# The pieces for sums of squares start at the fifth k-step of the first unit in the stage of seven products

## The chip, the cores and the metric

The kernel runs on one core of one Trainium2 chip. The time is that of one execution on the device, in microseconds (us). Three runs of the kernel before took 1785.42, 1786.99 and 1788.74 us, a median of 1786.99 us. The core has a matrix engine (PE, with its weight loads PEld as a row of their own), a vector engine (DVE), a scalar engine (ACT), a general engine (POOL), and a queue processor (SP) from which this kernel issues its DMA transfers.

## What is computed

One layer of an encoder over two groups of rows, 1024 "sample" rows and 256 "prompt" rows of 2048 features, each with 256 memory rows. The change concerns the scale of a root-mean-square norm, which is one number for each row of `x` and of `mem`:

```python
def rms_norm(x, g):
    xf = x.astype(jnp.float32)
    y = xf * lax.rsqrt(jnp.mean(xf * xf, axis=-1, keepdims=True) + EPS)
    return (y * g.astype(jnp.float32)).astype(x.dtype)

def layer(x, mem, norm_g, w_in, ..., w_out):
    hn = rms_norm(x, norm_g)
    proj = hn @ w_in
    xbc, z_ssd, dt_raw, q, k, v, z_att, mq, z_mem = split_cols(proj, IN_SIZES)
    ...
    memn = rms_norm(mem, mem_norm_g)
    mk, mv = split_cols(memn @ w_mem_kv, (MEM_WIDTH, MEM_WIDTH))
    ...
    return x + jnp.concatenate([o_ssd, o_att, o_mem], axis=-1) @ w_out
```

## The kernel before

Rows are handled in tiles of 128: ten of `x` (tiles 0 to 4 are the first group, 5 to 9 the second) and four of `mem`. Products are made in a split form: a weight or an activation is stored as a high part and a low part (`wh` and `wl`, `sh` and `sl`, `xH` and `xL`, `tH` and `tL`), and each product is three matmuls (lines 1240, 1241, 1242 in the stage of interest). `wsplit` (lines 206 and 207) makes the high part on ACT and the low part on DVE.

The order of the program is: keys and values of the memory rows, the block `q`, then **the stage of seven products**, and after that the attention, the scan, the gates and the output product.

**The stage of seven products** makes 14 units (`UNITS`), numbered u0 to u13 here. Each unit makes two blocks of 128 output features for the first and the second group of rows by seven products in place of eight. A unit has eight k-steps, and a k-step has 21 matmuls (seven products of three). The steps k=6 and k=7 are made product by product, so that each product ends in turn and its result is carried out while the others still run. `block_pair` loads the four weight blocks of a k-step (256 KB, tile `wraw`, line 1201), POOL makes three sums of them (tile `ws`, four instructions on line 1208), and `wsplit` makes `wh` and `wl` from `wraw`, `sh` and `sl` from `ws`. The tiles `wh` and `wl` have four buffers, `sh`, `sl` and `ws` three, `wraw` four. At the end of a unit `ev_seven` carries out the seven results; it begins with `yu`, an ACT copy (line 1330), and the rest is on DVE (lines 1332 to 1342). What is still to be done to a unit's results is put in the list `left` and done in small steps beside the next unit: a gate (`th`, stored to `zT` or `yT`) after u0, u2, u4 and so on, a convolution (`c` on line 362, `u` on line 368, stored to `xbc_d` on line 370) after u1, u3, u5 and so on up to u11.

**The pieces for sums of squares.** `stage_stats` goes through four tiles of `mem` and the tiles 5 to 9 of `x`, in pieces of 128 by 512: 36 pieces, four for a tile. For each piece there is a load (line 1392, tile `sst`), and an ACT instruction that squares it and sums along the row (line 1383). After the fourth piece of a tile DVE adds the four sums into `rx` (line 1386), and POOL makes the reciprocal root (lines 123 and 124). The pieces are in groups of three: a group takes four calls of `next(squares)`; the first call loads a piece, the second and third square one and load the next, the fourth squares the last. All pieces have one buffer, the tag `xst`, which they share with `wraw0` (the first weight block of the stage) ahead of them and with `yu` at the end of each unit. So a load waits for the square before it, the next group's first load waits until the last reader of `yu` is done (line 1340), and the very first load waits until `wraw0` has been split. The results `rx` are first read after the stage (`mk_prep`, `x_rows` of the second group).

**What sets the order.** The instructions of each engine are in a list that a scheduler makes: it takes the program as written, gives some parts a higher priority (`tc.high_priority`, used for the splits and for carrying out results), and lets an instruction go ahead of others where its own model of the engines says that it can start. Each engine then goes through its list strictly in order. DMA transfers are issued from the SP list in the same way: an issue that has to wait keeps all those behind it waiting.

The loop that the change touches, lines 1538 to 1554:

```python
    squares = stage_stats()
    owe = 0.0
    for u, unit in enumerate(units):
        for k in block_pair(w_in_pairs, u, rows_in, ev_seven(*unit), lead=2):
            if k in (0, 2, 4, 5):
                next(squares, None)

            owe = owe + (1.4 if k < 7 else 0.0) if left else 0.0
            while owe >= 1:
                owe -= 1
                if left:
                    some_left()
```

## Time and profile before

| what | us |
|---|---|
| median of three runs (lowest, highest) | 1786.99 (1785.42, 1788.74) |
| the profiled execution's own time | 1787.65 |
| its span, first to last instruction | 1785.9 |
| PE busy in the span | 1774.8 |
| DVE, ACT, POOL busy in the span | 1245.0, 921.6, 546.5 |

The seven products run from about 148.8 to 495.2 us of the span. The granted clock is 1.00 in this execution. Views of the trace are read as follows: a line of the timeline gives start, duration, engine, line and operation, the tiles written and read, how many such instructions in a row, and in brackets the idle time of the engine before it and what ended that; two numbers in a stretch's row are the engine's busy time and, in brackets, how many instructions it had. The ends of matmuls are modelled, and one starts before the one before it has ended: in the stage they start 0.146 us apart where nothing is waited for, though each is shown as some 0.31 us long.

### The profile page before, as it was taken

The numbers are of one execution on the slowest core, as the hardware profiler recorded it, in microseconds if no ns is written. First come the engines' busy times: TensorE is split into PE (matmuls) and PEld (weight loads), VectorE is DVE, ScalarE is ACT, GpSimd is POOL, SyncE is SP. The second block draws the span as 40 slices with busy tenths as digits, with TensorE's granted clock in tenths as the row PEclk, the third lists the DMA queues.
The fourth block names the chain that finished last, engine by engine and source line by source line (L and its number), as shares of the span: only waits on it lengthen the run. The fifth ranks groups of instructions, "written<-read, shape, count | busy, mean of one in ns | idle before, by whom it ended". The sixth has DMA issues, their size and how long they took to land.

```text
span 1785.9 us, 31408 instructions
## 1 busy us (share of the span) xinstructions
PE 1774.8 (99%) x10838; PEld 1606.1 (90%) x10838; DVE 1245.0 (70%) x2358; ACT 921.6 (52%) x2049; POOL 546.5 (31%) x900
## 2 busy tenths in 40 slices
PE   9999999999999999999999999999999999999999
PEld 7888999999998989999889977877988888899999
DVE  5596788888868877878665666557777644766665
ACT  5554455554434766756464565544447533533333
POOL 0105898988810100001001000000100000057775
PEclk9999999999999999999999999999999999999999
DMA  8554454445446644453635645557777754644442
GB/s 294 198 181 122 138 154 148 141 141 164 123 145 209 194 136 140 133 162 111 191 115 174 193 148 161 165 162 247 229 231 237 245 189 142 224 147 142 148 142 78
DMA packets 208207, 301.12 MB, mean 169 GB/s; under 512 B 19568, under 2 KB 86192, under 8 KB 208048
## 3 DMA queue, kind: packets, MB, share of 16 engines
q1 hardware_dynamic: 207904, 299.06, 54.0%
q8 instruction: 85, 1.39, 0.3%
q14 instruction: 74, 0.61, 0.1%
q10 hardware_dynamic: 144, 0.06, 0.0%
HBM read 236.36 MB, written 62.69 MB: 167 GB/s over the span
## 4 chain that ended last, share of the span: by engine, by line
PE 83%; DVE 5%; issue 5%; DMA 3%; POOL 2%; ACT 1%; SPq 0%; POOLq 0%; ACTq 0%; DVEq 0%
PE acc L258 9%; PE acc L260 9%; PE acc L259 9%; PE acc L1242 7%; PE acc L1240 7%; PE acc L1241 7%; PE acc L293 5%; PE acc L295 5%; PE acc L294 5%; PE accm L1241 3%; PE accm L1240 3%; PE accm L1242 3%; PE po L673 1%; PE ppt L663 1%; DVE wl L207 1%
## 5 line engine op out<-in xcount | busy, mean ns | idle before, releaser
L207 DVE TENSOR_TENSOR wl<-wraw,wh 128x512 fp32r<-128x512 f32 (+1 forms) x480 | 345.2, 721 | 244.0 <-ACT wh L206 234.9
L206 ACT ACTIVATE wh<-wraw 128x512 fp32r<-128x512 f32 (+1 forms) x480 | 292.2, 613 | 312.1 <-PE acc L260 148.4
L258 PE MATMUL acc<-wh,xH 128*128 128x512 f32 (+1 forms) x1088 | 418.7, 385 | 0.4 <-DVE v_all L337 0.4
L260 PE MATMUL acc<-wh,xL 128*128 128x512 f32 (+1 forms) x1088 | 410.0, 377 | 0.0
L259 PE MATMUL acc<-wl,xH 128*128 128x512 f32 (+1 forms) x1088 | 409.6, 376 | 0.0
L258 PEld LDWEIGHTS acc<-wh,xH 128*128 128x128 f32 x1088 | 204.5, 188 | 37.9 <-issue 3.3
L260 PEld LDWEIGHTS acc<-wh,xL 128*128 128x128 f32 x1088 | 204.2, 188 | 36.9 <-issue 0.2
L259 PEld LDWEIGHTS acc<-wl,xH 128*128 128x128 f32 x1088 | 204.7, 188 | 36.0 <-issue 1.6
L293 PE MATMUL acc<-xH,wh 128*128 128x320 f32 x640 | 202.7, 317 | 0.0
L294 PE MATMUL acc<-xL,wh 128*128 128x320 f32 x640 | 198.9, 311 | 0.0
L206 ACT ACTIVATE sh<-ws 128x384 fp32r<-128x384 f32 x176 | 91.3, 523 | 208.1 <-POOL ws L1208 108.9
L295 PE MATMUL acc<-xH,wl 128*128 128x320 f32 x640 | 198.0, 309 | 0.0
L207 DVE TENSOR_TENSOR sl<-ws,sh 128x384 fp32r<-128x384 f32 x176 | 124.4, 710 | 96.3 <-ACT sh L206 92.4
L1208 POOL TENSOR_TENSOR ws<-wraw 128x128 f32<-128x128 f32 x176 | 111.8, 635 | 209.0 <-DMA wraw<-in_w_in_pairs_dram 89.4
L635 POOL COPY lg<-nsink 128x2 f32<-128x2 f32 x40 | 13.8, 346 | 379.3 <-PE ppt L663 245.8
L293 PEld LDWEIGHTS acc<-xH,wh 128*128 128x128 f32 x640 | 120.2, 188 | 2.6 <-issue 2.2
L294 PEld LDWEIGHTS acc<-xL,wh 128*128 128x128 f32 x640 | 120.3, 188 | 1.7 <-issue 1.4
L1208 POOL TENSOR_TENSOR ws<-wraw,ws 128x128 f32<-128x128 f32 x176 | 117.5, 668 | 13.8
L295 PEld LDWEIGHTS acc<-xH,wl 128*128 128x128 f32 x640 | 120.2, 188 | 0.6 <-issue 0.5
L1208 POOL TENSOR_TENSOR ws<-ws,wraw 128x128 f32<-128x128 f32 x176 | 117.0, 665 | 0.0
L1208 POOL TENSOR_TENSOR wraw<-wraw 128x128 f32<-128x128 f32 x176 | 111.8, 635 | 13.7
L362 DVE SCALAR_TENSOR_TENSOR c<-u,vec,c 128x638 f32<-128x638 f32 (+1 forms) x96 | 90.0, 939 | 9.4 <-ACT c L357 9.0
(437 smaller groups left out, 3941.2 us busy)
## 6 DMA issues: line engine op xcount, KB each, us to landing
wraw<-in_w_in_laid_dram SPq DMA_DIRECT2D x176, 256.0 KB, 2.9
wraw<-in_w_in_pairs_dram SPq DMA_DIRECT2D x112, 256.0 KB, 2.7
wraw<-in_w_out_laid_dram SPq DMA_DIRECT2D x64, 256.0 KB, 3.3
wraw<-in_w_out_pairs_dram SPq DMA_DIRECT2D x64, 256.0 KB, 2.8
rf<-ac SPq DMA_DIRECT2D x40, 256.0 KB, 4.2
rb<-ac SPq DMA_DIRECT2D x40, 256.0 KB, 4.9
wraw<-in_w_mem_laid_dram SPq DMA_DIRECT2D x32, 256.0 KB, 4.7
xst<-in_x_sample_dram SPq DMA_DIRECT2D x20, 256.0 KB, 5.1
```

What stands on the lines that cost most here:

```text
L206: a = A.activation(h, raw, AF.Copy)
L207: b = V.tensor_sub(l, raw, h.bitcast(F32))
L258: T.matmul(ps[t][:, :n], sh, h[:, :n], start=(k_ == 0), stop=False)
L259: T.matmul(ps[t][:, :n], sh, l[:, :n], start=False, stop=False)
L260: T.matmul(ps[t][:, :n], sl, h[:, :n], start=False, stop=(k_ == KT - 1))
L293: T.matmul(o, sh, cur["H", q][:, m, c], start=(k == 0), stop=False)
L294: T.matmul(o, sh, cur["L", q][:, m, c], start=False, stop=False)
L295: T.matmul(o, sl, cur["H", q][:, m, c], start=False, stop=(k == KT - 1))
L1208: G.tensor_tensor(out=o, in0=x, in1=y, op=op)
L1240: T.matmul(ps[p], h, xh, start=(k_ == 0), stop=False)
L1241: T.matmul(ps[p], h, xl, start=False, stop=False)
L1242: T.matmul(ps[p], l, xh, start=False, stop=(k_ == 7))
```

## The change

In the first unit the calls of `next(squares)` at k=0 and k=2 are left out; those at k=4 and k=5 stay. In all other units the four calls stay as they were.

```diff
     for u, unit in enumerate(units):
         for k in block_pair(w_in_pairs, u, rows_in, ev_seven(*unit), lead=2):
-            if k in (0, 2, 4, 5):
+            if k in (4, 5) or u and k in (0, 2):
                 next(squares, None)
```

There are as many calls as the 36 pieces need, since there were 56 and are 54, and 48 do the work. By the written order each group of three now begins at k=4 of a unit and ends at k=2 of the next. What comes out in the engines' lists is shown at three places, in rows that give the line, the operation, the tiles written and read, and the shape. PE's list is the same in both.

The first place is ACT's list at the passage from the block `q` into u0. `qs` carries out the results of block `q`, `wh` and `sh` are splits for the seven products, `L1383` is a square, `tH` a part of the input rows. The piece of the difference:

```order
 L206 ACTIVATE wh<-wraw_1334 128x512
 L326 ACTIVATE qs<-acc 128x512 x2
-L1383 ACTIVATE sst,xs_1634<-sst 128x512
+L1383 ACTIVATE sst,xs_1752<-sst 128x512
 L326 ACTIVATE qs<-acc 128x512 x2
 L206 ACTIVATE wh<-wraw_1393 128x512
 L206 ACTIVATE wh<-wraw 128x512
 L326 ACTIVATE qs<-acc 128x512
-L1383 ACTIVATE sst,xs_1634<-sst 128x512
+L1383 ACTIVATE sst,xs_1752<-sst 128x512
 L206 ACTIVATE sh<-ws 128x384
 L1290 ACTIVATE tH<-ra 128x640
```

The two squares stand in the same two places as before, between the copies of `q` (only the number of the tile that takes the sums differs). The square that stood a few rows further on, third in u0, is no longer there; it comes next in u1.

The second place is SP's list just behind it: the stores of `q`, loads of weights (`wraw`), loads of pieces (`sst`), and the first store of a gate (`zT`).

```order
 L327 DMA q_126<-qs 128x512
 L327 DMA q_127<-qs 128x512
-L1201 DMA wraw<-in_w_in_pairs_dram 128x512
-L1392 DMA sst<-in_mem_sample_dram 128x512
-L1201 DMA wraw<-in_w_in_pairs_dram 128x512 x6
+L1201 DMA wraw<-in_w_in_pairs_dram 128x512 x7
 L1392 DMA sst<-in_mem_sample_dram 128x512
 L1366 DMA zT_0_118<-th 128x640
```

One load of a piece has gone from between the weight loads of u0; the first two loads, ahead of these rows, stand where they stood. All later pieces take the place of the one before, so that u1 to u11 have three each as before, and u12, which had none, has one.

The third place is u3, and the units u5, u7, u9 and u11 have the same: there the rest of a convolution and a gate fall together. First SP's list before,

```order
L1392 DMA sst<-in_mem_prompt_dram 128x512
L1201 DMA wraw<-in_w_in_pairs_dram 128x512 x3
L1392 DMA sst<-in_mem_prompt_dram 128x512
L370 DMA xbc_d<-u 128x638
L1366 DMA zT_0_118<-th 128x640
L1201 DMA wraw<-in_w_in_pairs_dram 128x512
L1392 DMA sst<-in_mem_prompt_dram 128x512
L1366 DMA zT_0_118<-th 128x640
```

and SP's list now:

```order
L1392 DMA sst<-in_mem_prompt_dram 128x512
L1201 DMA wraw<-in_w_in_pairs_dram 128x512 x3
L370 DMA xbc_d<-u 128x638
L1392 DMA sst<-in_mem_prompt_dram 128x512
L1366 DMA zT_0_118<-th 128x640
L1201 DMA wraw<-in_w_in_pairs_dram 128x512
L1366 DMA zT_0_118<-th 128x640
L1392 DMA sst<-in_mem_prompt_dram 128x512
```

The second load of a piece in the unit has moved behind the store of the convolution, and the third behind the second store of the gate. ACT's list in the same unit, as a piece of the difference:

```order
-L1383 ACTIVATE sst,xs_2415<-sst 128x512
-L206 ACTIVATE sh<-ws 128x384
-L206 ACTIVATE wh<-wraw 128x512
-L206 ACTIVATE sh<-ws 128x384
-L1383 ACTIVATE sst,xs_2415<-sst 128x512
-L206 ACTIVATE wh<-wraw 128x512
+L206 ACTIVATE sh<-ws 128x384
+L1383 ACTIVATE sst,xs_2621<-sst 128x512
+L206 ACTIVATE wh<-wraw 128x512
+L206 ACTIVATE sh<-ws 128x384
+L206 ACTIVATE wh<-wraw 128x512
+L1383 ACTIVATE sst,xs_2621<-sst 128x512
```

The second and the third square each stand one split later. On DVE the nine additions of the four sums (line 1386) move with their squares, from u1, u2, u3, u5, u6, u7, u9, u10, u11 to u1, u2, u4, u5, u6, u8, u9, u10, u12, and POOL's reciprocal roots with them. Behind the stage the lists are the same.

## The prediction

> **What bounds the kernel now.** I read the page first, then the busy times of three stretches (before the steady part of the seven products, the rest of that stage, and everything behind it).
>
> ```profile
> span 1785.9 us, 31408 instructions
> PE 1774.8 (99%) x10838; PEld 1606.1 (90%) x10838; DVE 1245.0 (70%) x2358; ACT 921.6 (52%) x2049; POOL 546.5 (31%) x900
> 148.80:153.20 4.40, 3.24 (x18) 2.47 (x17) 1.29 (x2) 3.38 (x8) 0.00 (x0) 1.00 0.63 196
> 153.20:495.20 342.00, 341.88 (x2338) 341.27 (x2337) 275.48 (x407) 171.39 (x342) 289.78 (x442) 1.00 0.47 141
> 495.20:1785.90 1290.70, 1282.21 (x7844) 1140.26 (x7842) 872.03 (x1790) 665.54 (x1551) 238.74 (x418) 1.00 0.55 171
> ```
>
> In a stretch's row the pairs are PE, PEld, DVE, ACT, POOL. PE is busy 1774.8 of 1785.9 us: no edit that leaves its work alone can win more than the 11.1 us between them. Inside the stage that the change touches, PE lacks 0.12 us of 342.00 once it runs, and 1.16 us of the first 4.40. So the stage is bound by PE, with one visible hole, at its start. The changed order has the same list on PE, so only holes can be filled or made.
>
> The hole in PE's own timeline, with the first matmul of the stage, the two that waited and the sixteenth:
>
> ```profile
> 148.79 0.30 PE L1240 MATMUL acc<-xH,wh 128*128 128x320 f32 x1
> ...
> 150.17 0.43 PE L1240 MATMUL acc<-tH,sh 128*128 128x320 f32 x1 [0.34 <-ACT qs L326]
> ...
> 152.40 0.42 PE L1240 MATMUL acc<-xH,sh 128*128 128x320 f32 x1 [0.82 <-ACT qs L326]
> ...
> 152.95 0.31 PE L1240 MATMUL accm<-tH,wh 128*128 128x320 f32 x1
> ```
>
> From the first to the sixteenth there are 15 steps, which took 152.95 - 148.79 = 4.16 us. At the stage's pace of 0.146 us (342.00 us by 2338 matmuls) they would take 2.19. So 1.97 us are lost here by the starts (the busy time says 1.16, because ends are modelled). PE waited for ACT to copy out the results of block q. Why ACT was late stands in its own timeline, with the SP rows of the loads:
>
> ```profile
> 144.91 0.60 ACT L326 ACTIVATE qs<-acc 128x512 f32<-128x512 f32 x1 [0.76 <-PE acc L260]
> 148.91 0.63 ACT L1383 ACTIVATE sst<-sst 128x512 f32<-128x512 f32 x1 [3.40 <-DMA sst<-in_mem_sample_dram]
> ...
> 149.54 1.28 ACT L326 ACTIVATE qs<-acc 128x512 f32<-128x512 f32 x2
> ...
> 151.76 0.59 ACT L326 ACTIVATE qs<-acc 128x512 f32<-128x512 f32 x1
> 153.15 0.63 ACT L1383 ACTIVATE sst<-sst 128x512 f32<-128x512 f32 x1 [0.80 <-DMA sst<-in_mem_sample_dram]
> ...
> 156.99 0.63 ACT L1383 ACTIVATE sst<-sst 128x512 f32<-128x512 f32 x1 [0.32 <-DMA sst<-in_mem_sample_dram]
> ...
> 145.54 0.33 SPq L1392 DMA_DIRECT2D sst<-in_mem_sample_dram  x1
> ...
> 153.90 0.33 SPq L1392 DMA_DIRECT2D sst<-in_mem_sample_dram  x1
> ```
>
> The first square stands in ACT's list between two copies of q. Its load was issued at 145.54, it started at 148.91, and ACT sat idle for 3.40 us with three copies behind it.
>
> **The change, part by part.** *First unit, first two pieces.* By its text the change takes these two squares out of the copies' way. The order of ACT's list says otherwise: the scheduler puts the first two squares into the same two places, and the two loads into the same places of SP's list. Then the load is issued at 145.54 again, the square waits 3.40 us again and PE loses the same 1.97 us. The bounds are -1.97 (all of it comes back) and 0; I take 0, since nothing ahead of these rows differs.
>
> *First unit, third piece.* One load (0.33 us of SP at 153.90) and one square (0.63 us, and 0.32 us of idle ahead of it) leave u0. Behind 153.20 PE has next to nothing to get: 0.12 us in all the rest of the stage. 0.
>
> *Units u1 to u11, even ones.* Each place for a piece is used by the next piece, three for a unit as before. Same loads, same squares, 0.
>
> *Units u3, u5, u7, u9, u11.* Here the second load moves behind the store of the convolution, and the third square behind one more split. I work it out in u3, in the order SP, DVE, ACT, PE:
>
> ```profile
> 231.17 0.42 SPq L1392 DMA_DIRECT2D sst<-in_mem_prompt_dram  x1
> 231.74 0.33 SPq L370 DMA_DIRECT2D xbc_d<-u  x1
> 235.72 0.33 SPq L1392 DMA_DIRECT2D sst<-in_mem_prompt_dram  x1
> ...
> 230.64 1.08 DVE L368 SCALAR_TENSOR_TENSOR u<-u,c 128x638 f32<-128x638 f32 x1
> 240.41 0.16 DVE L1386 TENSOR_REDUCE rx<-xs 128x1 f32<-128x4 f32 x1 [2.10 <-ACT sst L1383]
> 242.29 0.68 DVE L207 TENSOR_TENSOR wl<-wraw,wh 128x512 fp32r<-128x512 f32 x1
> ...
> 234.97 0.63 ACT L1383 ACTIVATE sst<-sst 128x512 f32<-128x512 f32 x1 [1.96 <-DMA sst<-in_mem_prompt_dram]
> 239.65 0.63 ACT L1383 ACTIVATE sst<-sst 128x512 f32<-128x512 f32 x1 [2.07 <-DMA sst<-in_mem_prompt_dram]
> 240.28 0.62 ACT L206 ACTIVATE wh<-wraw 128x512 fp32r<-128x512 f32 x1
> 240.80 0.51 ACT L206 ACTIVATE sh<-ws 128x384 fp32r<-128x384 f32 x1
> 241.22 0.62 ACT L206 ACTIVATE wh<-wraw 128x512 fp32r<-128x512 f32 x1
> ...
> 243.54 0.31 PE L1242 MATMUL acc<-xH,wl 128*128 128x320 f32 x1
> ```
>
> The store has to wait for `u`, done at 230.64 + 1.08 = 231.72, and takes 0.33 from 231.74. So the load that stood ahead of it at 231.17 goes out at 232.07, 0.90 us later. The square at 234.97, the load at 235.72 that waits for it, and the square at 239.65 all come up to 0.90 later, the last at 240.55. Before, a `wh`, a `sh` and the `wh` of the last k-step followed this square, the last one 241.22 - 239.65 = 1.57 us behind it. Now the first `wh` goes ahead of it, which saves 240.80 - 240.28 = 0.52. The last `wh` starts at 240.55 + 1.05 = 241.60, 0.38 us late, and its `wl` would end at 242.29 + 0.68 + 0.38 = 243.35. PE takes it at 243.54: still in time in u3, by 0.19 us. The tightest such place is in u7:
>
> ```profile
> 341.17 0.69 DVE L207 TENSOR_TENSOR wl<-wraw,wh 128x512 fp32r<-128x512 f32 x1
> ...
> 341.68 0.31 PE L1241 MATMUL acc<-xL,wh 128*128 128x320 f32 x1
> 341.91 0.41 PE L1242 MATMUL acc<-xH,wl 128*128 128x320 f32 x1
> ```
>
> `wl` ends at 341.86 and the matmul starts at 341.91, 0.23 us behind the one before it where 0.146 is usual. There is 0.05 us in hand, so 0.38 late costs PE 0.33. I count +0.33 for u7 and 0 for the other four, which I take to be nearer u3. Bounds: 0 (the store's wait is covered) and, with 0.90 late and 0.05 in hand in all five, 5 x 0.85 = +4.25.
>
> *The sums on DVE and POOL.* The nine additions stay nine. Three of them made DVE wait, the one in u3 for 2.10 us; the new order puts none at those three places. What PE could get from that is bounded by what it ever waited for a split:
>
> ```profile
> DVE rx L1386 <- ACT sst L1383: 4.4, 3, 2.1
>   PEld acc L1242: 0.6, 2
> 445.60:470.60 25.00, 24.88 (x170) 24.54 (x169) 22.66 (x31) 11.12 (x21) 22.94 (x33) 1.00 0.36 109
> ```
>
> DVE waited 4.4 us in three places, but the weight loads waited for `wl` or `sl` only 0.6 us in two. Bounds -0.6 and 0; I take 0, since the last split of those units hangs on the square and not on the addition. In u12 (445.60 to 470.60) a load, a square and an addition of 0.16 us are new. PE lacks 0.12 us there already, so DVE has nothing in hand: +0.1, with 0 and 0.16 as bounds.
>
> **Sum.** 0 + 0.33 + 0 + 0.1 = +0.4 us. On the profiled execution (1787.65, of which 1785.9 is the span) that is 1788.05; it stands 0.66 above the median of 1786.99, so against the median the forecast is 1787.4 us.
>
> A rule is weighed apart from this. The `wl` of one shape takes between two times, and POOL's sums too:
>
> ```profile
> L207 DVE TENSOR_TENSOR wl<-wraw,wh x112: 458/944/978, 151.4 to 489.6; 128x512 fp32r<-128x512 f32 x111, 128x288 fp32r<-128x288 f32 x1
> L1208 POOL TENSOR_TENSOR ws<-ws,wraw x106: 451/772/1044, 158.1 to 483.4; 128x128 f32<-128x128 f32 x106
> ```
>
> The Trainium skill's page "SBUF — State Buffer", section "Who interferes with whom", says that a DVE instruction with two inputs in SBUF and a POOL instruction that reads SBUF shut each other out for a whole instruction. The two modes of these rows agree with it. It speaks against a small change of places: by it a `wl` that comes 0.38 us later can meet another POOL instruction and take 0.94 in place of 0.46 us, and the sum by it would be 0.49 more, 1787.9 us; without it 1787.4.
>
> **The rivals.** *Slower: the last splits of u3, u5, u7, u9 and u11 come too late.* It decides from the point where the full 0.90 us reach the last `wl`, with u7's 0.05 us in hand. For it: the load cannot go ahead of the store any more, and PE has 0.12 us of holes in 342.00, so nothing absorbs a late split later. Against it: a `wh` has moved ahead of the square, and u3 has 243.54 - 242.97 = 0.57 in hand. Price +4.25: 1791.2 us.
>
> *Faster at the start: the squares come free of the copies after all.* For it: the 1.97 us are the largest hole of the stage, and the change's text moves just this. Against it: the two squares' places in ACT's list. Price -1.97: 1785.0 us. That is not outside 0.2% of 1786.99 (3.6 us), which is about what a measurement of this kernel can tell from no change.
>
> *Faster elsewhere.* Behind the stage PE lacks 1290.70 - 1282.21 = 8.49 us. If transfers there fell differently and half of it went, the time would be 1782.7 us. For it: this is where the holes are. Against it: the lists behind the stage are the same and the stage ends as it did.
>
> **How the numbers follow.** The forecast has 0.68, the slower rival 0.13, the faster start 0.13, the gain elsewhere 0.06. Around the forecast alone I expect 1785.4 to 1789.4: the three runs before spread over 3.3 us, and the small terms over 1. The range over all reaches down to the faster start and up to most of the slower rival: 1784.3 to 1790.8. Faster by over 0.2% is the gain elsewhere, 0.06; slower by over 0.2% is the slower rival, 0.13; within 0.2% the forecast and the faster start, 0.81.
>
> **What would show it.** The first square should again show an idle time of about 3.4 us on ACT, and PE two waits for `qs` at 150 and 152 us; if they are gone, my first step is wrong and the start gains up to 2 us. In u0 there should be two squares, in u12 one. In u3 the second load should come at about 232.1 and the third square near 240.5. PE's busy time from 153.2 to the end of the stage should stay within about 0.5 us of the stretch; a lack of 2 us or more, with waits for `wl` at the last k-step of u3 to u11, is the slower rival. A change of more than 1 us behind the stage would be something that I have not seen.

## The result and the profile after

The changed kernel took 1790.57 us (median of 7 runs, 1789.30 to 1793.80) against 1786.86 us for the kernel before on the same chip: a ratio of 1.0025, 95% interval 1.0015 to 1.0036. It is slower by about a quarter of a per cent. Measured a second time, for an experiment below, it stood at 1.0016 (1.0008 to 1.0025). In medians the loss is 3.7 us and, the second time, 3.2 us (1789.28 against 1786.09): small, but clear of the noise.

The page of the profiled execution and the same three stretches as before (PE, PEld, DVE, ACT, POOL: busy time and instructions; then granted clock, DMA share, GB/s):

```profile
span 1788.9 us, 31407 instructions
PE 1775.6 (99%) x10838; PEld 1606.0 (90%) x10838; DVE 1244.4 (70%) x2358; ACT 921.9 (52%) x2049; POOL 546.9 (31%) x900
```

```profile
148.80:153.20 4.40, 3.59 (x24) 3.29 (x23) 1.29 (x2) 3.57 (x9) 0.00 (x0) 1.00 0.66 228
153.20:495.20 342.00, 339.54 (x2311) 337.42 (x2310) 272.12 (x404) 170.65 (x339) 290.01 (x442) 1.00 0.47 140
495.20:1788.90 1293.70, 1285.01 (x7865) 1143.20 (x7863) 874.46 (x1793) 665.64 (x1551) 238.59 (x418) 1.00 0.55 170
```

The span grew by 3.0 us and PE's busy time by less than 1. In the steady part of the stage PE now lacks 342.00 - 339.54 = 2.46 us where it lacked 0.12. The stage as a whole, first to last matmul, took

```profile
148.94:498.13 349.19, 345.92 (x2352) 343.54 (x2351) 275.18 (x409) 174.32 (x347) 290.01 (x442) 1.00 0.47 140
```

which is 349.19 us, and 346.25 before (148.79 to 495.04, the first and the last of its 2352 matmuls). That is 2.94 us, the whole growth of the span. Where in the stage the time went shows when it is cut at the first matmul of each unit. A unit has 168 matmuls, 24.55 us at the pace of the stage. In the kernel before every unit from u1 to u11 took between 24.54 and 24.74, and u12 25.02. After, the units u4, u7, u8, u9, u11 and u12, in this order, are these:

```profile
248.20:273.31 25.11, 24.81 (x170) 24.55 (x169) 21.24 (x33) 12.32 (x26) 21.43 (x32) 1.00 0.47 128
...
322.44:347.77 25.33, 25.08 (x171) 24.55 (x169) 19.71 (x29) 13.57 (x28) 23.26 (x38) 1.00 0.50 154
347.77:372.96 25.19, 24.80 (x170) 24.54 (x169) 21.32 (x33) 12.50 (x26) 21.05 (x32) 1.00 0.42 127
372.96:398.91 25.95, 25.09 (x171) 24.57 (x169) 19.81 (x32) 13.29 (x28) 23.86 (x38) 1.00 0.51 152
...
423.45:448.54 25.09, 24.81 (x170) 24.55 (x169) 19.09 (x27) 13.62 (x28) 21.82 (x37) 1.00 0.57 169
448.54:473.73 25.19, 24.80 (x170) 24.54 (x169) 21.32 (x32) 11.06 (x22) 21.51 (x32) 1.00 0.40 119
```

The first column is the unit's length; above 24.55 they add up to 4.56 us, 2.72 in the odd units and 1.84 in the even ones. (The busy column shows less of it than the lengths do, because the modelled end of a matmul that waited is drawn out.) The first unit gave 0.9 us back in this execution, 25.63 for 26.53, which the repeats below show to be chance.

**An odd unit, u9.** First SP and ACT before, where the unit began at 371.97, then after, where it began at 372.96:

```profile
378.57 0.42 SPq L1392 DMA_DIRECT2D sst<-in_x_prompt_dram  x1
379.15 0.33 SPq L370 DMA_DIRECT2D xbc_d<-u  x1
383.28 0.33 SPq L1392 DMA_DIRECT2D sst<-in_x_prompt_dram  x1
...
382.53 0.63 ACT L1383 ACTIVATE sst<-sst 128x512 f32<-128x512 f32 x1 [2.12 <-DMA sst<-in_x_prompt_dram]
386.89 0.63 ACT L1383 ACTIVATE sst<-sst 128x512 f32<-128x512 f32 x1 [2.28 <-DMA sst<-in_x_prompt_dram]
```

```profile
380.04 0.33 SPq L370 DMA_DIRECT2D xbc_d<-u  x1
380.41 0.43 SPq L1392 DMA_DIRECT2D sst<-in_x_sample_dram  x1
385.58 0.33 SPq L1392 DMA_DIRECT2D sst<-in_x_prompt_dram  x1
...
384.83 0.63 ACT L1383 ACTIVATE sst<-sst 128x512 f32<-128x512 f32 x1 [1.32 <-DMA sst<-in_x_sample_dram]
390.73 0.63 ACT L1383 ACTIVATE sst<-sst 128x512 f32<-128x512 f32 x1 [3.72 <-DMA sst<-in_x_prompt_dram]
391.36 0.51 ACT L206 ACTIVATE sh<-ws 128x384 fp32r<-128x384 f32 x1
391.78 0.61 ACT L206 ACTIVATE wh<-wraw 128x512 fp32r<-128x512 f32 x1
...
392.42 0.90 DVE L207 TENSOR_TENSOR wl<-wraw,wh 128x512 fp32r<-128x512 f32 x1
...
392.44 0.41 PE L1240 MATMUL acc<-xH,wh 128*128 128x320 f32 x1 [0.48 <-ACT wh L206]
393.38 0.42 PE L1242 MATMUL acc<-xH,wl 128*128 128x320 f32 x1 [0.38 <-DVE wl L207]
```

Counted from the unit's start, the second load went out at 7.45 in place of 6.60, the second square started at 11.87 in place of 10.56, the third load at 12.62 in place of 11.31, the third square at 17.77 in place of 14.92. The third load leaves 0.75 us after the second square starts in both, because it needs the one buffer that the square frees. PE waits for the `wh` right behind the third square, and then for its `wl`.

This gives a rule that can be checked elsewhere. In u9 the third square started at 17.77 and 1.40 us were lost (25.95 - 24.55): the unit bears 16.37. In u11 it started at 440.36, 16.91 after the unit's start, and 25.09 - 24.55 = 0.54 was lost: 16.37 again. Over the odd units of the four profiles that have this order (the changed kernel, s1, r4 and g1 of the table below) the rule comes within 0.3 us of what was lost, so it is a rule of thumb, for this order alone.

How much u9 lost was partly chance. Its third load took 17.77 - 12.62 = 5.15 us to its square, against 3.61 before. With 3.61 the square would have started at 16.23, and by the rule nothing would have been lost. In the two profiles r4 and g1 of the same order it took 3.8 us, and u9 lost 0.14 and nothing.

u7 shows a second wait, near the unit's start. There PE waits for DVE to carry out the last results of the unit before (`r`, line 1340), and that stands in DVE's list behind a split that waited for ACT's `sh`, which is made of GpSimd's sums:

```profile
325.38 0.41 PE L1240 MATMUL accm<-tH,wh 128*128 128x320 f32 x1 [0.16 <-DVE r L1340]
...
323.81 0.78 DVE L207 TENSOR_TENSOR sl<-ws,sh 128x384 fp32r<-128x384 f32 x1 [1.05 <-ACT sh L206]
324.51 0.81 DVE L1340 TENSOR_TENSOR r<-accm,yu 128x640 f32<-128x640 f32 x1
```

By the starts of the matmuls, 0.41 of the 0.78 us of u7 are lost here. No unit of the kernel before had this wait.

**An even unit, u4.** GpSimd (POOL) after, 6 to 11 us behind the unit's start, with the DVE instruction that runs beside the first part of the root, and the matmul that waited later in the unit:

```profile
254.10 1.55 POOL L1208 TENSOR_TENSOR ws<-wraw 128x128 f32<-128x128 f32 x1 [2.58 <-DVE rx L1386]
255.74 0.65 POOL L123 TENSOR_SCALAR rx<-rx 128x1 f32<-128x1 f32 x1
256.46 0.80 POOL L1208 TENSOR_TENSOR wraw<-wraw 128x128 f32<-128x128 f32 x1
257.22 1.05 POOL L1208 TENSOR_TENSOR ws<-ws,wraw 128x128 f32<-128x128 f32 x1
258.23 0.55 POOL L124 TENSOR_TENSOR rx<-rx,mhalf 128x1 f32<-128x1 f32 x1
258.74 0.46 POOL L1208 TENSOR_TENSOR ws<-wraw,ws 128x128 f32<-128x128 f32 x1
259.16 0.46 POOL L1208 TENSOR_TENSOR ws<-wraw 128x128 f32<-128x128 f32 x1
...
255.26 1.08 DVE L362 SCALAR_TENSOR_TENSOR c<-u,vec,c 128x638 f32<-128x638 f32 x1
...
267.80 0.41 PE L1242 MATMUL acc<-xH,wl 128*128 128x320 f32 x1 [0.30 <-DVE wl L207]
```

The two instructions of a reciprocal root (lines 123 and 124), 128 numbers each, stand among the `ws` sums that make the next split weights. In the kernel before no root stood in u4, u8 or u12. From this I took two causes to the chip: late loads in the odd units, and roots in the even ones.

### The profile page after: what moved, and what is told of

Its sections match the earlier page's. It is cut to its first block, busy times and chain, and to the rows that moved or that the text cites. A ratio compares the mean times of both kernels' runs of the same rounds, so it can differ in the third digit from the quotient of the medians.

```text
span 1788.9 us, 31407 instructions
## 1 busy us (share of the span) xinstructions
PE 1775.6 (99%) x10838; PEld 1606.0 (90%) x10838; DVE 1244.4 (70%) x2358; ACT 921.9 (52%) x2049; POOL 546.9 (31%) x900
## 4 chain that ended last, share of the span: by engine, by line
PE 86%; POOL 5%; DVE 3%; DMA 3%; issue 2%; ACT 1%; SPq 0%; POOLq 0%; DVEq 0%; ACTq 0%
PE acc L258 12%; PE acc L260 12%; PE acc L259 12%; PE acc L1242 6%; PE acc L1240 6%; PE acc L1241 6%; PE acc L293 5%; PE acc L295 5%; PE acc L294 5%; POOL ws L1208 3%; PE accm L1241 2%; PE accm L1240 2%; PE accm L1242 2%; PE po L673 1%; PE ppt L663 1%
## 5 line engine op out<-in xcount | busy, mean ns | idle before, releaser
L1208 POOL TENSOR_TENSOR ws<-ws,wraw 128x128 f32<-128x128 f32 x176 | 121.2, 688 | 0.0
L1208 POOL TENSOR_TENSOR ws<-wraw,ws 128x128 f32<-128x128 f32 x176 | 114.9, 653 | 13.5
```

What stands on the lines that cost most here:

```text
L1208: G.tensor_tensor(out=o, in0=x, in1=y, op=op)
```

## The experiments

"Lost" is the time above 24.55 us (24.64 where the pace is that, as said below) in u1 to u12 of the run's one profile; "third square" is the mean start of the third square in u3, u5, u7, u9, u11 behind the unit's first matmul; u0 is the length of the first unit. The ratio is against the kernel before on the same chip, with its 95% interval. The runs were made on several chips: the kernel before took 1786.77 us beside s1 to s4, 1786.09 beside r1 to r4, 1786.41 beside q1, g1, p1 and p2, and 1786.72 beside h1 to h3. The last unit, u13, is not counted; it lost 0.5 us in s2 and 0.6 in r3.

| kernel | median us | ratio | u0 | lost | third square |
|---|---|---|---|---|---|
| before | 1786.86 | 1 | 26.53 | 0.7 | 15.0 |
| changed | 1790.57 | 1.0025 (1.0015 to 1.0036) | 25.63 | 4.6 | 16.8 |
| s1 two pieces earlier in u0, by the text | 1789.59 | 1.0016 (1.0007 to 1.0026) | 25.61 | 4.3 | 17.2 |
| s2 no piece in u0 | 1787.08 | 1.0003 (0.9994 to 1.0011) | 24.55 | 2.2 | 15.3 |
| s3 old places of the loads | 1788.11 | 1.0008 (0.9998 to 1.0017) | 25.63 | 3.0 | 15.4 |
| s4 sum once | 1787.40 | 1.0002 (0.9993 to 1.0012) | 25.71 | 0.5 | 15.5 |
| r1 root once | 1787.72 | 1.0010 (1.0001 to 1.0019) | 26.54 | 3.5 | 16.2 |
| r2 root twice | 1793.47 | 1.0046 (1.0034 to 1.0059) | 25.70 | 7.7 | 16.9 |
| r3 no piece in u0, sum once | 1785.48 | 0.9994 (0.9985 to 1.0003) | 24.64 | 0 | 13.9 |
| r4 changed, again | 1789.28 | 1.0016 (1.0008 to 1.0025) | 26.54 | 2.9 | 16.8 |
| q1 old places, root once | 1787.31 | 1.0002 (0.9993 to 1.0011) | 27.03 | 1.7 | 14.3 |
| g1 same order as changed | 1790.26 | 1.0018 (1.0009 to 1.0027) | 28.60 | 2.9 | 16.6 |
| p1 sum once, 256 bytes | 1787.77 | 1.0004 (0.9996 to 1.0013) | 28.45 | 0.5 | 15.4 |
| p2 no piece in u0, sum once, 256 bytes | 1784.13 | 0.9985 (0.9976 to 0.9994) | 24.55 | 0 | 13.5 |
| h1 no root in u4 and u8 | 1788.62 | 1.0009 (1.0000 to 1.0018) | 25.64 | 1.2 | 16.3 |
| h2 roots in u4, u8, u12 only, and one for the rest | 1787.43 | 1.0009 (1.0000 to 1.0018) | 25.61 | 1.7 | 16.3 |
| h3 old places, sum once | 1787.09 | 1.0004 (0.9995 to 1.0013) | 25.61 | 1.6 | 13.9 |

### Is it the place in the first unit, or what comes later?

```diff
-            if k in (4, 5) or u and k in (0, 2):
+            if k in (0, 2) or u and k in (4, 5):
```

> Only the place inside the first unit differs from the changed kernel: the two pieces of the first unit stand at its first and third k-step, not at its fifth and sixth. From the second unit on every piece is the same as in the changed kernel, one and a half tiles behind the kernel before. Theory A (the loss is made in the later units, by where the third load of an odd unit and the additions with their reciprocal roots have come to lie): the loss stays, 1790.6 us, within 1.5 us of the changed kernel, and TensorE loses its time again in u4, u5, u7, u8, u9, u11 and u12, 4.5 us there together. Theory B (the loss comes from where the first unit's squares lie): it goes back to 1787 us.

The loss stayed, 1.0016. But the edit did not change what it was meant to change: line by line, the lists of all five engines in this trace are those of the changed kernel, because the scheduler put the two pieces of u0 into the same places again. So the k-step in the program's text makes no difference, and what other places in u0 would cost was not tested. The run is a further measurement of the changed order, in which two pieces fewer are done in u0 and every later piece stands in another place. The units that lost were not those that I expected: u3 lost 1.25, u7 1.02, u9 1.55, u11 0.49, and u4, u5, u8, u12 nothing. Here are u3, u4 and u9:

```profile
223.63:249.43 25.80, 25.09 (x170) 24.57 (x169) 19.23 (x29) 13.45 (x28) 23.48 (x37) 1.00 0.49 151
249.43:273.98 24.55, 24.55 (x170) 24.55 (x169) 21.35 (x33) 12.63 (x26) 21.01 (x32) 1.00 0.43 132
...
373.19:399.29 26.10, 25.09 (x170) 24.57 (x169) 19.89 (x31) 12.99 (x28) 23.78 (x38) 1.00 0.50 149
```

The sum is nearly that of the first profile and the units differ. Where PE has stood still in u3, the other engines have gone on, and u4 then loses nothing. The order takes away the room; which unit pays is not settled by the order alone. For u9 the rule holds: its third square started at 391.11, 17.92 behind the unit's start, and 17.92 - 16.37 = 1.55.

```diff
-            if k in (4, 5) or u and k in (0, 2):
+            if u and k in (0, 2, 4, 5):
```

> No piece in the first unit; the four calls of every later unit stand where the kernel before has them, so the sequence is two tiles of it behind, and the loads of an odd unit have their old places on SP's queue (the third load behind the first zT store, not the second). The additions and roots come to the start of u2, u6 and u10 and elsewhere into the second and third pieces. Theory A1 (late loads in the odd units cost 2.75 us of the changed kernel): the odd units lose nothing beyond 0.4 us. Theory A2 (a root among the four ws instructions at the start of an even unit costs 0.6 us each): u2, u6 and u10 lose 0.6 us each, 1.9 us together, and u4, u8 and u12 nothing. The first hole of the stage shrinks by the square that stood between two copies of qs, 0.8 us or more. By A1 and A2 together 1787 us; by A1 alone 1785 us; by A2 alone 1790 us.

With no piece in u0 the first unit lost nothing at all, 24.55 us, and the time came to 1787.08, as the two causes together said (1785 by the first alone, 1790 by the second alone). In its units they were only roughly right: u2 and u6 lost 0.3 and 0.2 and u10 nothing, where 0.6 each was expected, and the odd units u3, u5 and u9 lost 1.5 together, where no more than 0.4 was expected. Even with the old places an odd unit can lose.

### Undoing one cause at a time

```diff
-            if k in (4, 5) or u and k in (0, 2):
+            for _ in range({0: 1, 2: 2, 4: 1}.get(k, 0) if u else k in (4, 5)):
                 next(squares, None)
```

> The first unit is that of the changed kernel; in each later unit the four pieces are called at other k-steps (one at the first, two at the third, one at the fifth), which puts the second and third load of an odd unit back to the places on SP's queue that the kernel before gives them, while the additions and the roots stay in the units where the changed kernel has them, and GpSimd's list is the changed kernel's to the row. Theory A1 (the loads' places on SP's queue make the last square of an odd unit late, 2.75 us in u5, u7, u9 and u11): 2.5 us less than the changed kernel, 1788 us, with u4, u8 and u12 still losing 1.9 us. Theory A2 alone (the roots at the start of u4, u8 and u12 make the loss, and the odd units only follow from a late GpSimd): 1790.6 us, no change, u5, u7, u9 and u11 still lose 2.7 us.

The third squares came back from 16.8 to 15.4, and the median to 1788.11, 1.5 us below s1, which is the changed order on the same chip. The intervals of the two ratios overlap, so this gain in time is not clear of the noise. But u3 still lost 0.81 and u7 1.16, with third squares at 16.08 and 16.56: with the old places one more split stands behind the third square, and these two units bore only 15.3 and 15.4 where the changed order bears 16.37. So a third square that comes 1.4 us earlier is worth less than 1.4 us. Of the 1.9 us that u4, u8 and u12 were expected to go on losing, 0.9 were lost.

```diff
                     x = pieces.pop(g + i - ahead)
                     A.activation(x, x, AF.Square, accum_out=s4[:, c:c + 1])
-                    if c == 3:
+                    if c == 3 and kept is None:
...
+        r = rx[:, 5:14]
+        V.reduce_sum(out=r, in_=kept, axis=AX.X)
+        rsqrt(r, r, 1.0 / D, 9)
```

> The pieces stand where the changed kernel has them, SP's order of loads and stores included, but the sums of the nine tiles are kept and added in one instruction, with one reciprocal root, behind the last piece in u12; the x tiles go first. So GpSimd has no root between its ws instructions from u1 to u11. Theory A2 (the roots at the start of u4, u8 and u12 cost 0.6 us each): u4 and u8 lose nothing and the time is 1.2 to 1.9 us under the changed kernel, 1789 us; u5, u7, u9 and u11 still lose 2.5 us. Theory A1 alone: no change, 1790.6 us. If the odd units' loss hangs on the roots too, it goes to 1787 us or below.

This was the surprise of the first four. With the loads still at the new places, but with no addition and no root on the way, u1 to u11 lost nothing, the odd units included. The loss needs the sums or the roots, and s4 stands 2.2 us below s1 on the same chip. (Its units are 0.09 us longer each, of which more below; p1, without that, loses nothing from u1 to u11 either.) The two that follow part sums and roots.

```diff
                         V.reduce_sum(out=r, in_=s4, axis=AX.X)
-                        rsqrt(r, r, 1.0 / D, 1)
+                        if root:
+                            rsqrt(r, r, 1.0 / D, 1)
```

> The changed kernel with its pieces, loads, stores, squares and the nine additions on VectorE where they are, but the nine reciprocal roots on GpSimd are left to one, over all nine columns, behind the last piece in u12. Theory R (the roots on GpSimd make the last weight splits late): as with the sum taken once, no time lost in u3 to u11, 1787.4 us, 3 us under the changed kernel. Theory S (the additions make it: VectorE does not start the split behind an addition until ScalarE's square is there): no change, 1790 us, with losses in several of u3, u4, u5, u7, u8, u9, u11, u12 as before.

With all nine additions in place, no unit from u1 to u11 lost anything but u9, and the median is 1.6 us below r4, the changed kernel on the same chip: it is the roots, and at most a little the additions. u9 lost 1.66 without a root, and its rows show how. The third load was issued at 383.77, 12.40 behind the unit's start and no later than usual, and took 5.63 us to the square, where 3.5 is common:

```profile
383.77 0.33 SPq L1393 DMA_DIRECT2D sst<-in_x_prompt_dram  x1
...
389.40 0.63 ACT L1383 ACTIVATE sst<-sst 128x512 f32<-128x512 f32 x1 [4.20 <-DMA sst<-in_x_prompt_dram]
```

It started at 18.03, and 18.03 - 16.37 = 1.66. The 1.82 us that u12 lost belong to the one root over nine columns, which came to stand at the start of u12; the second instruction of a root over nine columns took 1.81 us.

```diff
+                        if root == 2:
+                            rsqrt(sm.tile([P, 1], F32, tag="dbl", name="dbl", bufs=4), r, 1.0 / D, 1)
                         rsqrt(r, r, 1.0 / D, 1)
```

> The changed kernel with every reciprocal root of this stage done twice on GpSimd, the first time into a column that nobody reads. Theory R (what a root takes from GpSimd is lost one for one wherever the last split has no room left): a root took 1.2 us with its turn in u4, so each of the units that lost time (u4, u5, u7, u8, u9, u11, u12 in the profile of the changed kernel) loses about 1 us more, and the time is 5 to 8 us above the changed kernel, 1796 us. Theory S (not the roots): within 1 us of the changed kernel, 1790.6 us.

1793.47 us, 4.2 us more than the changed kernel on the same chip (r4, 1789.28), with intervals that do not overlap, and 7.7 us lost in u1 to u12. That bears out the theory of the roots, at half a microsecond for each doubled root. It is less than the 5 to 8 us that I expected: where a unit has room left, a root is still hidden.

> The changed kernel itself once more, for what a second profile of the same instructions shows. If each unit's loss hangs on the order alone, u4, u5, u7, u8, u9, u11 and u12 lose again what they lost in its first profile, 4.6 us together, each within 0.2 us. If the order only takes the room away, and what is then lost depends on when the weights land and how long GpSimd's instructions take, the sum stays between 3 and 6 us and other units lose.

The same list of instructions, in a second profile: u3 lost 0.32, u4 0.46, u7 0.81, u9 0.14, u11 1.12, and u8 and u12 nothing; the third squares at 16.8 as before. So a single profile says that the room is gone, not which unit pays. u0 took 26.54 us here and 25.63 in the first, so the 0.9 us that seemed regained was chance.

### Which roots, and do the places cost anything without them?

```diff
-                        rsqrt(r, r, 1.0 / D, 1)
+                        if root or t % 3 < 2:
+                            rsqrt(r, r, 1.0 / D, 1)
...
+        for c in (12, 6, 9):
+            rsqrt(rx[:, c:c + 1], rx[:, c:c + 1], 1.0 / D, 1)
```

> The changed kernel with three of its nine reciprocal roots, those at the start of u4, u8 and u12, left to u13; the six others stay. Theory C1 (these three cost the even units their last split, and make the first load of u5 and u9 late): nothing lost in u4, u8 and u12, u3, u7 and u11 still lose 0.5 to 1 us each, the time 1 to 1.5 us under the changed kernel, 1788.5 us. Theory C2 (all roots count alike, through how late GpSimd is as a whole): a third of the roots' part, about 0.8 us less, with losses still spread over even and odd units, 1789 us.

This told nothing of the roots: the scheduler put the three roots, which were ready, back where they had been, and the list was the changed kernel's on every engine (one `MEMSET` of DVE starts just ahead of a split in place of just behind it). It serves as another look at that order: 1790.26 us, 2.9 us lost in u3, u4, u7, u8, u10 and u11. To keep a root away, it has to lack its input. So the sums of the three tiles were kept, and added behind the last one:

```diff
+                    if late is not None and c0 <= tiles[t][1] < c0 + n9:
+                        s4 = late[:, tiles[t][1] - c0, :]
-                    elif c == 0:
...
+        r = rx[:, 5:8]
+        V.reduce_sum(out=r, in_=late, axis=AX.X)
+        rsqrt(r, r, 1.0 / D, 3)
```

> The changed kernel's places. The tiles are taken in another order, and the sums of the three whose addition stood at the start of u4, u8 and u12 are kept and added together, with one root, in u12; the additions and roots of the six others stay where the changed kernel has them. So the additions and the roots in u4 and u8 are gone, all else is in its place. Theory C1 (each root costs where it stands): u4 and u8 lose nothing; u3, u5, u7, u9 and u11 lose what their third square is later than 16.4 us, 1.5 to 2 us together. Theory C2 (only how late GpSimd is as a whole counts): two of nine roots less, all units lose a little less.

u4 and u8 lost nothing (24.55 each). GpSimd at the place shown above, without the root:

```profile
254.44 0.99 POOL L1208 TENSOR_TENSOR ws<-wraw 128x128 f32<-128x128 f32 x1 [2.61 <-DVE wl L207]
...
258.00 1.04 POOL L1208 TENSOR_TENSOR ws<-wraw 128x128 f32<-128x128 f32 x1
```

The wait ahead is as long, 2.61 for 2.58 us, so the addition that the changed kernel's row names was not what GpSimd waited for. From the first of these sums to the end of the fifth it took 259.04 - 254.44 = 4.60 us, and 259.62 - 254.10 = 5.52 with the root: 0.92 us for 128 numbers. The odd units kept 1.0 us of loss, u3 0.15, u7 0.28, u11 0.61, where 1.5 to 2 were expected. u7 lost its 0.28 with its third square at 16.34, in time by the rule: all of it in the wait for line 1340 near the unit's start.

The reverse keeps these three roots and leaves the six others to one in u10 (`c0=8, n9=6` in the same edit):

> The reverse: the additions and roots at the start of u4, u8 and u12 stay, the six others are kept and added together with one root in u10. Theory C1: u4, u8 and u12 lose 0.4 to 0.6 us each wherever the unit ahead of them lost nothing, 1.5 us together; the first load of u3, u7 and u11 is earlier than in the changed kernel (about 1 us behind the unit's start in place of 2 to 3 us) and these units lose nothing; u5 and u9 have their root just ahead of them still, and may lose up to 0.5 us. Theory C2: a third of the loss, spread over the units.

The units u3, u4 and u8:

```profile
222.81:247.36 24.55, 24.55 (x170) 24.55 (x169) 19.55 (x28) 12.72 (x27) 22.60 (x35) 1.00 0.51 158
247.36:272.39 25.03, 24.81 (x171) 24.55 (x169) 21.17 (x33) 12.52 (x26) 21.43 (x32) 1.00 0.43 128
...
346.03:370.85 24.82, 24.81 (x171) 24.55 (x169) 20.95 (x32) 12.55 (x26) 20.93 (x32) 1.00 0.43 130
```

u4 lost 0.48, u8 0.27, u12 0.26; u3, u5, u7 and u9 nothing. The first loads of u3 and u7 went out 1.17 and 1.30 us behind the unit's start, where the changed kernel has 2.05 and 2.91. u11 still lost 0.66, with its first load at 2.65: the root of six columns in u10 is just ahead of it. So each root costs at its place: at the start of an even unit it makes the last splits of that unit late, and near the end of an even unit it makes GpSimd, and with it the weight loads and the first piece's load behind them, late for the odd unit that follows.

The wait for line 1340 bears this out. By the starts of the matmuls it cost u7 0.38 to 0.53 us in the four profiles of the changed order, where a root stands some 5 us before the end of u6, and up to 0.51 in u11. With every root doubled (r2) it cost u7 0.97 and u11 1.04. In s2, whose roots stand near the end of u4 and u8, it came in u5 and u9. In the seven runs that take only one root, in u12, it never came.

```diff
-            if k in (4, 5) or u and k in (0, 2):
+            for _ in range({0: 1, 2: 2, 4: 1}.get(k, 0) if u else k in (4, 5)):
...
+        rsqrt(rx[:, 5:14], rx[:, 5:14], 1.0 / D, 9)
```

> Both suspects undone together: the loads of an odd unit at their old places on SP's queue, and the nine roots left to one, in u13; the additions, the squares and the first unit are the changed kernel's. Theory C (an odd unit loses what its third square starts later than 16.4 us behind the unit's first matmul; the new places make it 1.3 us later and the roots another 1 us): the third squares start at 14 to 15.5 us, no unit from u1 to u12 loses anything, and the time is that of the kernel before or up to 2 us less, 1785 to 1786.5 us. If something else is left (the additions, the later phase of the pieces as such): 1788 us or more with losses in u3 to u12.

Both undone: third squares at 13.4 to 15.2, and nothing lost from u1 to u11 but 0.1 in u10. u12 lost 1.6, because the scheduler put the root of nine columns at its start again and not into u13. Without that the median of 1787.31 would come to some 1785.7, about that of the kernel before (1786.41 on this chip), and within the 1785 to 1786.5 that were expected; measured it is above them.

> The first unit of the changed kernel, the loads of an odd unit at their old places on SP's queue, and the sum taken once with one root, kept in a tile of 256 bytes. Without roots the third square came at 15.1 to 16.0 us with the changed kernel's places, under 16.4 us, so the places should cost nothing any more: the same as the sum taken once on the changed kernel's places (1787.8 us with 256 bytes), within 1 us, its third squares at 13 to 14.5 us and nothing lost in u1 to u11. Against the same with no piece in the first unit (1784.1 us) it shows what the two pieces of the first unit cost: 1 to 3 us of hole in u0.

The same with the sum taken once: third squares at 13.9, nothing lost from u1 to u11, 1.6 in u12 from the one root. Four means of the third square now stand crosswise: 16.8 with the new places and the roots (16.6 to 17.2 in four profiles of this order of the later pieces), 15.4 with the old places and the roots (s3), 15.4 and 15.5 with the new places and no roots (p1 and s4), 13.9 with neither. The places make it 1.4 to 1.5 us later, the roots with their additions as much again. (With the roots alone away and the additions in place it is 16.2 in r1, u9's slow load included, and 14.3 in q1.) In time the two are not alike. Without the roots, u1 to u11 lose next to nothing with either places, the slow load of r1 aside; with the roots and the old places s3 still lost 3.0 us in its profile. So the roots are needed for the loss that comes back in every profile. That the new places add to it is likely but not shown: the lost times differ by 0.7 us (3.7 in the mean of four profiles against 3.0 in one) and the medians of s1 and s3 by 1.5, both within the noise.

### Both causes away, and a better kernel

> Two changes together: no piece in the first unit (the sequence two tiles behind the kernel before, the loads of an odd unit at their old places on SP's queue), and the sums of the nine tiles added once, with one root, behind the last piece. Theory R: neither the hole of the first unit (1.1 us in the changed kernel) nor the roots are left, so 3.5 to 4 us under the changed kernel, 1785.5 us to 1786 us. Theory A1 without the roots (the odd units' late loads are what counts): the same as without a piece in the first unit, 1787 us.

> As the sum taken once on the changed kernel's places, but the tile that keeps the sums has 256 bytes in each partition in place of 144, and the addition and the root come in u13. In the two runs with 144 bytes every unit took 24.64 us of matmuls where it takes 24.55 elsewhere. If that comes from how 144 bytes shift the tiles behind it: 24.55 us again, and with no loss in u12 the time is 1.8 us less than with 144 bytes, 1785.6 us. If it comes from something else of these kernels: 24.64 us again, 1786.9 us.

> No piece in the first unit and the sum taken once, with the keeping tile at 256 bytes in each partition. With no hole in the first unit, no loss in u1 to u12 and units of 24.55 us: 1.2 us under the same with 144 bytes, 1784.2 us, 2 us or a little more under the kernel before. If the units take 24.64 us again: 1785.5 us.

r3 puts the edits of s2 and s4 together. It came to 1785.48 us, where 1785.5 to 1786 was expected, but its units took 24.64 us each in place of 24.55, as those of s4 did. p1 is s4 with a larger tile for the sums, and p2 is r3 with that tile. The edit of p2 against r3 is only

```diff
-        kept = sm.tile([P, 9, 4], F32, tag="kept", name="kept", bufs=1)
+        kept = sm.tile([P, 16, 4], F32, tag="kept", name="kept", bufs=1)[:, :9]
```

and the whole stage of p2, first to last matmul, is

```profile
148.30:491.80 343.50, 343.50 (x2352) 343.50 (x2351) 273.64 (x401) 175.45 (x347) 277.29 (x426) 1.00 0.46 142
```

PE lacks nothing in 343.50 us. The kernel takes 1784.13 us, where 1784.2 was expected, 0.9985 of the kernel before (0.9976 to 0.9994). p1 had its pace back as expected, but its median of 1787.77 did not fall to the 1785.6 expected: its profile lost 3.9 us in u0, more than the 1.1 of s4, and one profile cannot say how often that happens. The runs without a piece in u0 spread less, p2 from 1782.20 to 1785.01 in 11 runs and the kernel before from 1783.92 to 1790.19 in the 33 beside it.

## Why the prediction was wrong

*The bound and the first unit* were right. The stage is bound by PE, only holes could be made, and what lies behind it did not change. The two squares stood between the copies again, as the prediction read from ACT's list:

```profile
148.16 0.63 ACT L1383 ACTIVATE sst<-sst 128x512 f32<-128x512 f32 x1 [2.51 <-DMA sst<-in_mem_sample_dram]
```

ACT waited 2.51 us in place of 3.40, in a list that is the same so far, and in the repeat u0 took as long as before. The terms of 0 for the first unit stand. The rival *faster at the start* asked for the right thing in the wrong kernel: the change left two squares there, and s2, with none, won the 2 us of u0.

*Units u3, u5, u7, u9 and u11* is the first step that failed, by its size: +0.33 us was counted, "0 for the other four, which I take to be nearer u3". In the four profiles with this order of the later pieces (changed, s1, r4, g1) the odd units lost 2.75, 4.31, 2.39 and 2.05 us, 2.9 in the mean, against 0.2 before. The form was right: the second load goes behind the store of the convolution, one `wh` less stands behind the third square, and the first `wl` after it is what PE waits for. The shift of the third square was not. The prediction took 0.90 us at most for it; the trace has 1.78 (16.79 - 15.01, the means of the five units). Of these, 0.60 are the load's new place behind the store, less than the 0.90 reckoned. The other 1.18 were not priced: 0.53 because the second piece now takes 4.35 us from issue to square in place of 3.82; 0.36 because the third takes 3.96 in place of 3.60; 0.29 because the first load is itself later. (In the mean of the four profiles the third square is 1.84 later, and the parts are 0.74, 0.42, 0.31 and 0.37.) The third load's move behind the gate's second store cost nothing, since it leaves 0.75 us after the second square starts in both kernels. In the kernel before the third squares started at 15.24, 13.88, 16.12, 14.92 and 14.87; 1.78 later, and held against 16.37, they give 0.65, 0, 1.53, 0.33 and 0.28, together 2.8 us. The sum fits, the units do not: u3 lost nothing and u9 1.40 in the profile of the result. Nor had u7 the 0.05 us in hand that the prediction read: its matmul at 341.91 already came 0.23 us behind the one before it in place of 0.146, and u7 took 24.73 us in the kernel before. So working out each unit's margin was the right tool, but it was done with half of the shift and with the margins of two units for all five.

*The sums on DVE and POOL* is the second step that failed, and the larger one, in what it left out. It priced the addition, 0.16 us, and not the root behind it:

```profile
L124 POOL TENSOR_TENSOR rx<-rx,mhalf 128x1 f32<-128x1 f32 x9 | 5.0, 551 | 0.4
L123 POOL TENSOR_SCALAR rx<-rx 128x1 f32<-128x1 f32 x9 | 3.6, 400 | 0.8
```

Nine roots take 8.6 us of GpSimd in a stage where it is busy 290 of 342 us, as the stretch row above shows. They were there before, with 9.4 us; what is new is where they stand. Three of them moved to the start of u4, u8 and u12, which the step *even ones* put at 0: "same loads, same squares". These units lost 1.84 us in the profile of the result, but 0, 0.46 and 0.71 in the three others. In the mean that is 0.75, against 0.5 before in u12 that the change took away. So the even units add little to the result on average; h1 and h2 show that the roots are what they pay for. Through the first load of the next unit, and through the wait for line 1340, the roots also cost the odd ones: without roots and additions (s4, p1) these lose nothing with the new places, and with roots and the old places (s3) they still lost 2.1 us. So more of the odd units' loss hangs on the roots than on the places that the prediction reckoned with.

Odd units 2.7 us more, even units about 0.3 more: 3.0 us, against the 3.7 and 3.2 measured. The *slower* rival had the right place, the right wait and the sign, with 1791.2 us against 1790.57. Its stated point, the full 0.90 us reaching the last `wl`, is not how it came about, and that its time lies so close is luck: it took 0.85 us in each of five units, where the four profiles show three or four units with 0.1 to 1.6 us. It was given 0.13, because "u3 has 0.57 in hand" was set against it, and that was one unit's margin against 0.38 us; the chance should have followed from all five and from what the chain behind the load could add.

The rule weighed beside the forecast, the Trainium skill's page "SBUF — State Buffer", section "Who interferes with whom", agrees with the rows of u4 above. A root's first instruction took 0.65 us there, while an instruction of the convolution with more than one input ran on DVE (255.26 to 256.34), and 0.19 in u2, where DVE stood idle:

```profile
217.53 0.19 POOL L123 TENSOR_SCALAR rx<-rx 128x1 f32<-128x1 f32 x1
...
218.04 0.56 DVE L207 TENSOR_TENSOR sl<-ws,sh 128x384 fp32r<-128x384 f32 x1 [0.91 <-ACT sh L206]
```

The 0.49 us that the prediction took from this rule for one `wl` is far from the 3 us of the result. It was not applied to the roots, where these two rows differ by 0.46 us; how much of the loss that makes is not shown.

## What to carry to other kernels

Before a list of side work is shifted by some steps, work out the room at the tightest wait of every period, not of one, and reprice the whole chain (issue, landing, the wait for a single buffer, the next issue), because each link's delay comes on top. Count what follows an instruction too: a reduction to 128 numbers brought two GpSimd instructions that made GpSimd 0.92 us later at a bad place. Work that nobody reads until later is best collected and done once, at a place with room, and one profile shows that room is gone, but not which period will pay for it.

## What the runs showed of the hardware

**The clock fell to half behind two waits of 1 us or less, in some executions.** In g1 PE waited 1.03 and 0.81 us for the copies of q in the first unit, and then ran for 3 us at half its clock. The stretch around the waits and the two behind it:

```profile
149.00:152.50 3.50, 1.71 (x9) 0.93 (x7) 0.97 (x2) 3.32 (x7) 0.00 (x0) 0.97 0.51 145
152.50:153.00 0.50, 0.44 (x2) 0.44 (x3) 0.33 (x1) 0.01 (x1) 0.00 (x0) 0.50 0.98 377
153.00:155.50 2.50, 2.50 (x11) 2.50 (x11) 0.93 (x2) 2.17 (x5) 0.00 (x0) 0.50 0.79 275
```

The granted clock is 0.97, 0.50 and 0.50, and 11 matmuls in 2.50 us are 0.23 us apart in place of 0.146. The first unit took 28.60 us for it. The same happened in p1 (28.45), with waits of 0.72 and 0.82 us, and not in q1, with 0.87 and 0.82. That the waits are the cause is not shown by a run that varies them. The Trainium skill's page "TensorE: Matmul & The Clock Gate", section "What's actually happening", describes a window of 3.4 us that runs freely, and an idle window as what throttles. That agrees with a drop that comes in some executions and not in others; but PE was busy for 1.71 of the 3.50 us ahead here, so it did not need a window that is idle throughout.

**144 bytes changed PE's pace.** r3 and p2 differ only in the size of the tile that keeps the sums, 144 or 256 bytes in a partition. With 144 every unit took 24.64 us, with 256 it took 24.55, over the whole stage 1.3 us, and the medians, on two chips, differ by 1.35. The same two lengths came in s4 (144) and p1 (256). That the tiles behind it are shifted, and PE's reads with them, is a guess; no run moved one operand alone.

**A load's landing varied by 2 us.** The third piece of an odd unit, 256 KB behind a queue of weights and stores, took from 2.9 (u7 of r4) to 5.7 us (u9 of s1) from issue to square in the same list. In u9 of r1 it alone decided that the unit paid, and in u9 of the changed kernel too, by the rule above. What it collided with was not found.
